# Moving low parts and the sine products of a rotation from GpSimd to VectorE in one layer of a decoder trunk

## The chip, the cores and the metric

The kernel runs on one core of one Trainium2 chip. The metric is the device time of one execution in microseconds, the median of several runs. The engines are named as in the profile: PE is TensorE (PEld its weight loads), DVE is VectorE, ACT is ScalarE, POOL is GpSimd, SP is SyncE, which issues most transfers.

## The reference

One layer of a trunk is computed for 2048 prompt rows and 8 single sample rows of width 1024, all in 32-bit floats:

```python
mod = (jax.nn.silu(c) @ w_ada + b_ada)[:, None, :]
sh1, sc1, g1, sh2, sc2, g2 = jnp.split(mod, 6, axis=-1)
h = modulate(x, norm1_g, sh1, sc1)          # rmsnorm(x, gain) * (1 + scale) + shift
u, q, k, v, a_pool, a_attn = project_inputs(h, pos, w_in, q_norm_g, k_norm_g)
# q, k: per-head rmsnorm, then rope:
#   concatenate([x1 * cos - x2 * sin, x2 * cos + x1 * sin], axis=-1)
pool_y = pool_mix(ext, pos, w_pool_grp, pool_scale)
# three groups of 4 heads with (window, dilation) = (128,1), (512,4), (2048,16)
attn_y = combine_groups(outs, lses)
merged = sigmoid(a_pool) * (pool_y @ w_pool_br) + sigmoid(a_attn) * (attn_y @ w_attn_br)
x = x + g1 * (merged @ w_out)
h2 = modulate(x, norm2_g, sh2, sc2)
x = x + g2 * (jnp.square(jax.nn.relu(h2 @ w_up)) @ w_down)
```

## The kernel before

Everything is held transposed, with features on the 128 partitions and positions along the free dimension. The positions are worked in two groups (`ci` 0: 1024 prompt rows and the 8 sample rows; `ci` 1: the other 1024 prompt rows), each in two halves of 512 or 520 columns.

Products keep the precision of 32-bit floats by splitting each operand into a high part, which is the value rounded to the matmul's type (fp32r), and a low part, which is the rest. A matmul becomes three (high x high, high x low, low x high), added up in PSUM (`mm3`, L156). So every weight tile is loaded by SyncE into a raw buffer, cast by ScalarE to its high part, and a subtraction makes its low part (`load_w`, L178 to 185). Its default engine is GpSimd (`eng=G`); the tiles of `w_ada` have VectorE. `weights` (L213) hands the tiles out in the order of `plan` (L188 to 207) and asks for the next one or two ahead of use (`depth`), and passes GpSimd. There are three raw buffers and three for the parts. The same split is made for the modulated rows h and h2 in `modulated` (L317): VectorE multiplies x by the reciprocal root, ScalarE scales and shifts, ScalarE casts the high part, and the low part is made on GpSimd for odd k and on VectorE for even k (calls at L360 and L1252).

The stages are: an opening (L748), in which the first blocks of `w_ada`, the norm of x and the first q/k tiles are made as the data lands; the first group's q/k/v projection (`qkv`, L393), gates with the rest of `w_ada` and the sample rows' attention beside them, the pooling branch (L530); the second group's pooling branch; its q/k/v projection with the attention of all heads interleaved (L929 to 1141); its gates with the merging of the heads; then for each group the output projection (`project`, L1254), the second norm (`norm2`, L1246), and the two feed-forward products (`up`, `down`), which take the second half of the time.

In `qkv` each chunk of q or k is copied out of PSUM by ScalarE as a pair of half-heads `a`, `b` and as squares. `after_qk` (L400) then adds the two squares on GpSimd (L405), makes the products with sine on GpSimd (L409, L411) and with cosine on VectorE (L410, L412), a difference and a sum on VectorE (L413, L414), and some microseconds later the norm over a head by a small matmul, square root and reciprocal (L416 to 422). The result is split into high and low parts in `ohl` (one buffer; ScalarE L444, GpSimd L445) and stored; the attention reads it back later.

TensorE's order of work is written out by hand: the class `Order` (L65) keeps a running estimate of TensorE's time and steps through generators with delays, so that small matmuls and other stages are laid between the large ones. The order on each of the other engines' queues is chosen when the program is built, by priority; `first()` (L149) raises it, for weights (L182) and for the copies out of PSUM. On each engine instructions run in their queue's order.

Of the kernel before, what the change touches and what calls it, by code (L numbers as in the profile page):

```python
# [8 lines left out]
F32 = mybir.dt.float32  # L9
F32R = mybir.dt.float32r  # L10
AF = mybir.ActivationFunctionType
ALU = mybir.AluOpType
# [4 lines left out]
P = 128  # L17
# [97 lines left out]
def emit(tc, I, O):  # L115
    nc = tc.nc
    V, S, G, PE, SP = nc.vector, nc.scalar, nc.gpsimd, nc.tensor, nc.sync
# [90 lines left out]
    ready = []  # L208
    extra = []
    issued = [0]  # L210
    depth = [DEPTH]

    def weights(*key):  # L213

        i = issued[0] - len(ready)
        assert plan[i] == key, (plan[i], key)
        while issued[0] < len(plan) and issued[0] <= i + depth[0]:
            k = plan[issued[0]]
            src = I[k[0]][k[1]] if len(k) == 2 else I[k[0]][k[1], :, k[2] * 1024:(k[2] + 1) * 1024]
            ready.append(load_w(src, G, *(extra if issued[0] == 3 else ())))  # L220
            issued[0] += 1
        return ready.pop(0)

# [5 lines left out]
    for name, shape in CPACK:  # L229
        n = int(np.prod(shape))  # L230
# [83 lines left out]
            V.reciprocal(out=rs[:, c0:c0 + n], in_=rs[:, c0:c0 + n])  # L314
        return rs

    def modulated(hf, x, xr, rs, n, i, k, dst, c0, samp, eng):  # L317

        sh = (0 if i == 0 else 24) + k
        V.tensor_tensor(out=xr, in0=x, in1=rs[:, :n], op=ALU.mult)  # L320
        S.activation(out=hf[:, :n], in_=xr, func=AF.Identity, scale=sc[:, i, k, 0:1], bias=mod[:, sh, 0:1])
        if samp:
            sl = slice(n - NS, n)
            V.tensor_tensor(out=hf[:, sl], in0=xr[:, sl], in1=sc[:, i, k, 1:9], op=ALU.mult)
            V.tensor_tensor(out=hf[:, sl], in0=hf[:, sl], in1=mod[:, sh, 1:9], op=ALU.add)
        S.copy(out=dst[:, k, 0, c0:c0 + n], in_=hf[:, :n])
        eng.tensor_tensor(out=dst[:, k, 1, c0:c0 + n], in0=hf[:, :n], in1=dst[:, k, 0, c0:c0 + n].bitcast(F32), op=ALU.subtract)  # L327


    ph1 = ExitStack()  # L330
# [25 lines left out]
    def make_h(ci, hi, xs, rs, hb, ks=range(KD)):  # L356
        c0, n, splits = HALVES[ci][hi]
        for k in ks:
            hf = npl.tile([P, 520], F32, tag="sq", bufs=3, name="hf")
            modulated(hf, xs[k], xs[k], rs, n, 0, k, hb, c0, ci == 0 and hi == 1, G if k % 2 else V)  # L360

    def subs(ci):
        out = []
# [29 lines left out]
    def qkv(ci, hb, done=None):  # L393
        st = ExitStack()
        opened = None if ci else opening()
        ap = pool(st, f"qkv{ci}", side="left")
# [3 lines left out]
        def after_qk(g, qk, t0, n, ab, sq):  # L400
# [5 lines left out]
            a, b, co, si = ab[:, 0, :n], ab[:, 1, :n], cs[:, 0, :n], cs[:, 1, :n]  # L406
            t = ap.tile([P, 2, 512], F32, tag="rt", bufs=1, name="rt")
            o = ap.tile([P, 2, 512], F32, tag="ro", bufs=2, name="ro")
            G.tensor_tensor(out=t[:, 0, :n], in0=b, in1=si, op=ALU.mult)  # L409
            V.tensor_tensor(out=o[:, 0, :n], in0=a, in1=co, op=ALU.mult)  # L410
            G.tensor_tensor(out=t[:, 1, :n], in0=a, in1=si, op=ALU.mult)  # L411
            V.tensor_tensor(out=o[:, 1, :n], in0=b, in1=co, op=ALU.mult)  # L412
            V.tensor_tensor(out=o[:, 0, :n], in0=o[:, 0, :n], in1=t[:, 0, :n], op=ALU.subtract)  # L413
            V.tensor_tensor(out=o[:, 1, :n], in0=o[:, 1, :n], in1=t[:, 1, :n], op=ALU.add)  # L414
# [5 lines left out]
            V.reciprocal(out=rs[:, :n], in_=rs[:, :n])  # L420
            for i in range(2):
                V.tensor_tensor(out=o[:, i, :n], in0=o[:, i, :n], in1=rs[:, :n], op=ALU.mult)
            ohl = ap.tile([P, 2048], F32R, tag="ohl", bufs=1, name="ohl")
            dst = (kst if qk else qst)[g]
            for i in range(2):
                oi = o[:, i, :npr]
# [819 lines left out]
    def norm2(ci, hi, acc, hb, xa):  # L1246
        c0, n, splits = HALVES[ci][hi]
        yield 2500
        rs = rms_finish(tp, stp, acc, splits)
        for k in range(KD):  # L1250
            hg, hf = wtile("hg"), wtile("hf")
            modulated(hf, xa[k][:, c0:c0 + n], hg[:, :n], rs, n, 1, k, hb, 0, ci == 0 and hi == 1, G if k % 2 else V)  # L1252

    def project(ci, hi, hb, xa, load_xa=None):  # L1254
        c0, n, splits = HALVES[ci][hi]
# [65 lines left out]
    for ci in range(2):  # L1321
# [4 lines left out]
        xa = []  # L1326
# [9 lines left out]
        accs = tp.tile([P, KD, NS], F32, tag="accs", bufs=1, name="accs") if ci == 0 else None  # L1336
        br = od.spawn(branches(ci, 1, hbs[1], GAP_B), 3000)
        depth[0] = DEPTH_O
        acc = project(ci, 0, hbs[0], xa, load_xa)
        od.drain(br)  # L1340
        n0 = od.spawn(norm2(ci, 0, acc, hbs[0], xa))
# [139 lines left out]
```

## Time and profile before

| | |
|---|---|
| median of 3 runs | 3063.06 us (3058.80 to 3064.57) |
| profiled execution | 3062.32 us |
| its span, first to last instruction | 3060.5 us |
| TensorE busy | 2933.8 us, 96% |
| VectorE busy | 1590.5 us, 52% |
| ScalarE busy | 982.3 us, 32% |
| GpSimd busy | 966.2 us, 32%, of which 649.3 us at L184 |
| chain that ended last, by engine | PE 76%, DMA 5%, DVE 5%, issue 4%, POOL 3%, ACT 2% |

Busy shares are means over stages with different limits. The time of a matmul includes part of its neighbours' time, since they are pipelined. An idle time is put down to what ended it. "issue" is time in which an engine waited for nothing that the profile shows.

### The profile page before, as it was taken

To read this page: it belongs to the slowest core of one execution; us is meant where nothing else is said; L and a number is where in the kernel's file an instruction comes from. 1 tells how busy PE (TensorE), PEld (TensorE's weight loads), DVE (VectorE), ACT (ScalarE), POOL (GpSimd) and SP (SyncE) were. 2 spreads that over 40 slices of the span, in tenths; PEclk is the share of its full clock that TensorE was granted. 3 is DMA by queue.
4 is the path that set the end of the run, shared out by engine and by line. 5 is a ranking of instruction groups with operands and counts; after the bars stand their busy time and mean duration, and the time that the engine had idled before them with its cause. 6 is when DMAs were issued, how large, how long until landed. Compare 5 with 4: busy or idle time off the path is not lost.

```text
span 3060.5 us, 40917 instructions
## 1 busy us (share of the span) xinstructions
PE 2933.8 (96%) x16220; PEld 2510.3 (82%) x16220; DVE 1590.5 (52%) x2649; ACT 982.3 (32%) x1772; POOL 966.2 (32%) x510
## 2 busy tenths in 40 slices
PE   6899999999898799999999999999999999999999
PEld 3899788887787688878899999999877888888887
DVE  5556442541744534456865545555677554444444
ACT  5333342433554534433521221121235211111211
POOL 2665341433533312233532122122245312221221
PEclk7999999999999889999999999999999999999999
DMA  6544752335777779876321111111272211111111
GB/s 239 172 144 154 270 183 92 118 118 151 200 196 203 186 191 229 239 243 218 105 78 48 43 49 49 42 51 47 92 242 83 76 42 56 48 49 42 55 43 69
DMA packets 207599, 379.09 MB, mean 124 GB/s; under 512 B 47424, under 2 KB 103072, under 8 KB 206624
## 3 DMA queue, kind: packets, MB, share of 16 engines
q1 hardware_dynamic: 195888, 359.63, 38.6%
q10 hardware_dynamic: 11520, 16.85, 1.5%
q8 instruction: 128, 2.10, 0.3%
q14 instruction: 63, 0.52, 0.1%
HBM read 294.89 MB, written 81.75 MB: 123 GB/s over the span
## 4 chain that ended last, share of the span: by engine, by line
PE 76%; DMA 5%; DVE 5%; issue 4%; POOL 3%; ACT 2%; SPq 1%; ACTq 0%; DVEq 0%; POOLq 0%
PE ps_dn L153 23%; PE ps_up L153 22%; PE ps_g L153 10%; PE ps_v L153 4%; PE ps_qk L153 4%; PE ps_wo L153 3%; PE ps_u L153 3%; PE ps_o L153 1%; PE ps_pb L153 1%; POOL wh L184 1%; PE ps_s L153 1%; PE ps_ada L153 1%; DMA slab<-kst 1%; DMA cs<-in_rope 1%; PE ps_ab L153 1%
## 5 line engine op out<-in xcount | busy, mean ns | idle before, releaser
L184 POOL TENSOR_TENSOR wh<-wr,wh 128x1024 fp32r<-128x1024 f32 (+1 forms) x274 | 649.3, 2377 | 1637.9 <-ACT wh L183 1620.7
L153 PE MATMUL ps_dn<-rt,wh 128*128 128x512 f32 (+2 forms) x3840 | 727.0, 350 | 5.3 <-POOL wh L184 3.3
L153 PEld LDWEIGHTS ps_dn<-rt,wh 128*128 128x128 f32 x3840 | 619.6, 188 | 108.2 <-POOL wh L184 4.2
L183 ACT CAST wh<-wr 128x1024 fp32r<-128x1024 f32 (+1 forms) x306 | 309.4, 1023 | 737.9 <-issue 564.0
L1306 DVE SCALAR_TENSOR_TENSOR xa<-ps_dn,mod,xa 128x512 f32<-128x512 f32 (+1 forms) x640 | 405.2, 642 | 202.1 <-PE ps_dn L153 195.9
L153 PE MATMUL ps_g<-h,wh 128*128 128x512 f32 (+2 forms) x1920 | 389.6, 354 | 0.4 <-POOL wh L184 0.4
L153 PE MATMUL ps_up<-hb,wh 128*128 128x264 f32 (+2 forms) x2304 | 371.7, 319 | 0.0
L153 PE MATMUL ps_up<-ha,wh 128*128 128x512 f32 x1536 | 367.3, 395 | 0.0
L153 PEld LDWEIGHTS ps_up<-hb,wh 128*128 128x128 f32 x2304 | 332.3, 188 | 36.1
L153 PEld LDWEIGHTS ps_g<-h,wh 128*128 128x128 f32 x1920 | 307.2, 190 | 48.5 <-POOL wh L184 1.0
L153 PEld LDWEIGHTS ps_up<-ha,wh 128*128 128x128 f32 x1536 | 286.6, 188 | 66.3 <-issue 0.5
L153 PE MATMUL ps_qk<-h,wh 128*128 128x512 f32 (+2 forms) x1440 | 301.4, 362 | 14.2 <-POOL wh L184 4.9
L1290 DVE TENSOR_TENSOR r<-r 128x512 f32<-128x512 f32 (+2 forms) x160 | 99.3, 621 | 389.2 <-ACT r L1289 389.1
L153 PEld LDWEIGHTS ps_qk<-h,wh 128*128 128x128 f32 x1440 | 233.6, 193 | 58.5 <-POOL h L327 6.3
L1292 DVE TENSOR_TENSOR rt<-r,rt 128x512 fp32r<-128x512 f32 (+2 forms) x160 | 218.0, 1362 | 81.7 <-ACT rt L1291 81.6
L1289 ACT ACTIVATE r<-ps_up 128x512 f32<-128x512 f32 (+2 forms) x160 | 82.1, 513 | 416.8 <-PE ps_up L153 416.8
L153 PE MATMUL ps_v<-wh,h 128*128 128x256 f32 (+1 forms) x1224 | 171.6, 297 | 25.4 <-ACT wh L183 19.3
L153 PEld LDWEIGHTS ps_v<-wh,h 128*128 128x128 f32 (+1 forms) x1224 | 157.8, 195 | 30.5 <-ACT wh L183 19.7
L945 ACT ACTIVATE pe<-pe,ost 128x128 f32<-128x128 f32 (+1 forms) x192 | 87.1, 454 | 142.5 <-DVE ost L943 139.5
L943 DVE CUSTOM_DVE_ANT_0 pe<-ps_s,cp 128x128 f32<-128x128 f32 (+1 forms) x192 | 61.5, 358 | 118.2 <-PE ps_s L153 118.0
L1291 ACT CAST rt<-r 128x512 fp32r<-128x512 f32 (+2 forms) x160 | 85.7, 536 | 66.4 <-DVE r L1290 66.4
L445 POOL TENSOR_TENSOR ohl<-ro,ohl 128x256 fp32r<-128x256 f32 (+1 forms) x66 | 76.1, 1175 | 92.4 <-ACT ohl L444 81.8
(182 smaller groups left out, 2981.7 us busy)
## 6 DMA issues: line engine op xcount, KB each, us to landing
wr<-in_w_up SPq DMA_DIRECT2D x72, 512.0 KB
wr<-in_w_down SPq DMA_DIRECT2D x68, 512.0 KB
wr<-in_w_in SPq DMA_DIRECT2D x64, 512.0 KB
wr<-in_w_ada SPq DMA_DIRECT2D x48, 512.0 KB
slab<-kst SPq DMA_DIRECT2D x40, 512.0 KB
wr<-in_w_out SPq DMA_DIRECT2D x32, 512.0 KB
cs<-in_rope SPq DMA_DIRECT2D x18, 512.0 KB
qst<-ohl SPq DMA_DIRECT2D x9, 1024.0 KB
```

Source lines behind the costliest of these rows:

```text
L153: PE.matmul(ps, w, x, start=start, stop=stop)
L183: S.copy(out=wt[:, 0, :n], in_=raw[:, :n])
L184: eng.tensor_tensor(out=wt[:, 1, :n], in0=raw[:, :n], in1=wt[:, 0, :n].bitcast(F32), op=ALU.subtract)
L445: G.tensor_tensor(out=pl, in0=pi, in1=ph.bitcast(F32), op=ALU.subtract)
L943: V.tensor_tensor_reduce(out=pe[:, off:off + nk], in0=ps[:, off:off + nk], in1=mask[:, mo:mo + nk], scale=-0.125, scalar=3.0e38, op0=ALU.a ...
L945: S.activation(out=pe[:, off:off + nk], in_=pe[:, off:off + nk], func=AF.Exp, scale=-1.0, bias=o[:, 64:65], accum_out=o[:, 65:66])
L1289: S.activation(out=r1[:, :l], in_=ps[:, :l], func=AF.Relu)
L1290: V.tensor_tensor(out=r1[:, :l], in0=r1[:, :l], in1=r1[:, :l], op=ALU.mult)
L1291: S.copy(out=rt[:, 0, a:a + l], in_=r1[:, :l])
L1292: V.tensor_tensor(out=rt[:, 1, a:a + l], in0=r1[:, :l], in1=rt[:, 0, a:a + l].bitcast(F32), op=ALU.subtract)
L1306: V.scalar_tensor_tensor(out=x[:, c0 + a:c0 + a + lp], in0=ps[:, :lp], scalar=mod[:, 40 + m, 0:1], in1=x[:, c0 + a:c0 + a + lp], op0=ALU.m ...
```

## The change

Three kinds of operations go from GpSimd to VectorE. In `weights` the engine of the low part becomes a variable, VectorE until the first group's output projection begins, and GpSimd from there on (the tiles of `w_attn_br`, loaded in `branches`, keep the default). In `modulated` the low part is always on VectorE. In `after_qk` both sine products are on VectorE. Besides, `ohl` has two buffers in the first group and one, as before, in the second.

```diff
+    weng = [V]
...
-            ready.append(load_w(src, G, *(extra if issued[0] == 3 else ())))
+            ready.append(load_w(src, weng[0], *(extra if issued[0] == 3 else ())))
...
-    def modulated(hf, x, xr, rs, n, i, k, dst, c0, samp, eng):
+    def modulated(hf, x, xr, rs, n, i, k, dst, c0, samp):
...
-        eng.tensor_tensor(out=dst[:, k, 1, c0:c0 + n], in0=hf[:, :n], in1=dst[:, k, 0, c0:c0 + n].bitcast(F32), op=ALU.subtract)
+        V.tensor_tensor(out=dst[:, k, 1, c0:c0 + n], in0=hf[:, :n], in1=dst[:, k, 0, c0:c0 + n].bitcast(F32), op=ALU.subtract)
...
-            modulated(hf, xs[k], xs[k], rs, n, 0, k, hb, c0, ci == 0 and hi == 1, G if k % 2 else V)
+            modulated(hf, xs[k], xs[k], rs, n, 0, k, hb, c0, ci == 0 and hi == 1)
...
-            G.tensor_tensor(out=t[:, 0, :n], in0=b, in1=si, op=ALU.mult)
+            V.tensor_tensor(out=t[:, 0, :n], in0=b, in1=si, op=ALU.mult)
             V.tensor_tensor(out=o[:, 0, :n], in0=a, in1=co, op=ALU.mult)
-            G.tensor_tensor(out=t[:, 1, :n], in0=a, in1=si, op=ALU.mult)
+            V.tensor_tensor(out=t[:, 1, :n], in0=a, in1=si, op=ALU.mult)
...
-            ohl = ap.tile([P, 2048], F32R, tag="ohl", bufs=1, name="ohl")
+            ohl = ap.tile([P, 2048], F32R, tag="ohl", bufs=2 - ci, name="ohl")
...
-            modulated(hf, xa[k][:, c0:c0 + n], hg[:, :n], rs, n, 1, k, hb, 0, ci == 0 and hi == 1, G if k % 2 else V)
+            modulated(hf, xa[k][:, c0:c0 + n], hg[:, :n], rs, n, 1, k, hb, 0, ci == 0 and hi == 1)
...
         depth[0] = DEPTH_O
+        weng[0] = G
         acc = project(ci, 0, hbs[0], xa, load_xa)
```

## Rows read from the trace of the kernel before

**Rows 1.** Busy us of PE, PEld, DVE, ACT, POOL by stretch; clock; DMA
```profile
0.00:125.00 125.00, 90.51 (x480) 67.00 (x481) 73.71 (x101) 59.73 (x103) 55.30 (x43) 0.85 0.54 197
125.00:750.00 625.00, 608.86 (x3666) 524.42 (x3666) 276.05 (x364) 228.41 (x364) 257.25 (x153) 0.99 0.47 155
750.00:1150.00 400.00, 349.70 (x2015) 308.97 (x2014) 193.31 (x442) 189.84 (x445) 142.39 (x85) 0.93 0.78 198
1380.00:3060.50 1680.50, 1660.39 (x8840) 1420.57 (x8838) 938.09 (x1339) 411.24 (x628) 450.25 (x197) 1.00 0.22 74
```

**Rows 2.** Groups by shape, GpSimd to 1380 us, then VectorE: busy us, mean ns
```profile
L184 POOL TENSOR_TENSOR wh<-wr,wh 128x1024 fp32r<-128x1024 f32 x89 | 218.6, 2460 | 444.6 <-ACT wh L183 442.1 <-issue 2.4
L409 POOL TENSOR_TENSOR rt<-ab,cs 128x512 f32<-128x512 f32 x18 | 28.7, 1597 | 42.8 <-ACT ab L390 24.1 <-DMA cs<-in_rope 18.7
...
L413 DVE TENSOR_TENSOR ro<-ro,rt 128x264 f32<-128x264 f32 x6 | 2.6, 426 | 0.0
```

**Rows 3.** Timeline of VectorE and GpSimd: start us, length us, operation, idle before
```profile
311.98 1.23 DVE L184 TENSOR_TENSOR wh<-wr,wh 128x1024 fp32r<-128x1024 f32 x1 [2.35 <-ACT wh L183]
...
78.20 0.69 DVE L410 TENSOR_TENSOR ro<-ab,cs 128x512 f32<-128x512 f32 x1
...
83.47 1.71 POOL L405 TENSOR_TENSOR qsq<-qsq 128x512 f32<-128x512 f32 x1
83.99 1.75 DVE L414 TENSOR_TENSOR ro<-ro,rt 128x512 f32<-128x512 f32 x1
```

**Rows 4.** Timeline of TensorE in the opening, with what ended its idle time
```profile
39.35 3.72 PE L153 MATMUL ps_qk<-h,wh 128*128 128x512 f32 x8 [3.21 <-POOL wh L184]
...
54.97 4.63 PE L153 MATMUL ps_qk<-h,wh 128*128 128x512 f32 x10 [1.69 <-POOL wh L184]
...
86.93 5.60 PE L153 MATMUL ps_qk<-h,wh 128*128 128x256 f32 x32 [3.88 <-POOL h L327]
...
120.51 0.71 PE L153 MATMUL ps_hs<-qsq,cp 128*128 128x264 f32 x2 [2.52 <-POOL qsq L405]
```

**Rows 5.** Timeline of GpSimd, ScalarE and VectorE ahead of those four waits
```profile
33.30 3.23 POOL L327 TENSOR_TENSOR h<-hf,h 128x512 fp32r<-128x512 f32 x1 [32.87 <-ACT h L326]
...
43.36 1.16 ACT L305 ACTIVATE sq<-x 128x520 f32<-128x520 f32 x2 [3.71 <-POOL h L327]
...
51.13 3.42 DVE L314 RECIPROCAL rs<-rs 128x256 f32<-128x256 f32 x2 [1.36 <-ACT rs L313]
...
85.15 1.72 POOL L327 TENSOR_TENSOR h<-hf,h 128x520 fp32r<-128x520 f32 x1
...
118.85 0.91 POOL L411 TENSOR_TENSOR rt<-ab,cs 128x256 f32<-128x256 f32 x1
```

**Rows 6.** Timeline of TensorE from 750 to 1150 us, three of its waits
```profile
882.10 1.08 PE L153 MATMUL ps_o<-vt,px 128*128 128x64 f32 x8 [1.19 <-DVE ost L963]
...
925.80 4.42 PE L153 MATMUL ps_v<-wh,h 128*128 128x256 f32 x19 [2.77 <-POOL wh L184]
...
1068.82 0.79 PE L153 MATMUL ps_v<-wh,h 128*128 128x256 f32 x2 [16.22 <-ACT wh L183]
```

**Rows 7.** Timeline of VectorE and GpSimd ahead of the first two
```profile
878.26 3.49 DVE L422 TENSOR_TENSOR ro<-ro,qrs 128x512 f32<-128x512 f32 x2
878.26 2.93 POOL L184 TENSOR_TENSOR wh<-wr,wh 128x1024 fp32r<-128x1024 f32 x1 [2.64 <-ACT wh L183]
...
922.95 2.79 POOL L184 TENSOR_TENSOR wh<-wr,wh 128x1024 fp32r<-128x1024 f32 x1
```

**Rows 8.** Chain that ended last, around the third: start, length, what
```profile
1060.50 0.57 SPq L456
```

**Rows 9.** Timeline of VectorE and TensorE near 350 us
```profile
350.85 4.47 DVE L184 TENSOR_TENSOR wh<-wr,wh 128x1024 fp32r<-128x1024 f32 x2
354.25 1.47 PE L153 MATMUL ps_ada<-wh,silr 128*18 128x512 f32 x3 [3.82 <-DVE wh L184]
```

**Rows 10.** GpSimd's waits from 750 to 1150 us: what, total us, times, longest
```profile
POOL wh L184 <- ACT wh L183: 85.9, 8, 31.6
```

## Prediction

> **What bounds the kernel now.** I read four views in this order: the busy times by stretch, the timeline of TensorE with what ended its idle time, the timelines of the engines named there, and the groups by shape for prices. The stretches [rows 1] show a kernel that TensorE fills: after 1380 us it is busy 1660.39 of 1680.50 us, and little that VectorE or GpSimd do there can return time. Its idle time lies in two places, 34.5 us in the first 125 us (the opening) and 50.3 us from 750 to 1150 us (the second q/k/v projection, between whose matmuls the attention runs). From 125 to 750 us it idles 16.1 us. So the change is worth what it takes out of waits in the opening and in 750 to 1150 us, at most some 85 us, and much of that is first loads and waits on other engines.
>
> GpSimd is a slow place for these operations and it slows VectorE as well. A 128x1024 low part takes 2.46 us on GpSimd in the mean of 89, a sine product of 512 columns 1.60 us [rows 2]; VectorE, alone, does a 128x1024 low part in 1.23 us [rows 3]. A 128x512 operation takes 0.69 us on VectorE alone, but when GpSimd has one at the same moment the two take 1.75 and 1.71 us [rows 3]. That pair is done after about 1.73 us; both on VectorE would take 1.38.
>
> **The moved work.** Counted from the code: 87 weight low parts (42 of the first group, 44 of the second, and the first output-projection tile, fetched before the switch at L1340); 32 of the 64 low parts of modulated rows (odd k), 16 before 1150 us and 16 after 1380; 60 sine products (30 chunks of two), 36 of 512 columns and 24 of 256 or 264. On VectorE, alone: 87 x 1.23 = 107 us, 32 x 0.69 = 22 us, 36 x 0.69 + 24 x 0.43 = 35 us (0.43 from a sum of 264 columns [rows 2]). That is 164 us, of which 138 fall before 1150 us (75 weights, 16 rows, all products), where VectorE is busy 543 of 1150 us [rows 1]. It comes to 59%, less what it gains by fewer collisions; 750 to 1150 us goes from 193 to some 240 of 400 us, the opening from 74 to some 95 of 125 us (7 weights, 8 rows, 12 products). No stretch becomes full. GpSimd loses over 300 us. Busy time is not the question; order and latency are. Each moved low part still waits for ScalarE's cast (L183, L326), now in VectorE's queue, where the copies of ps_v (L510), ps_o (L963) and the score reductions (L943) stand behind it; TensorE waits for all three.
>
> **The opening, step by step** [rows 4].
> (a) At 39.35 us TensorE resumes after 3.21 us, released by a weight's low part. GpSimd had first spent 3.23 us on a modulated row, from 33.30, and came to the weights at 36.5 [rows 5]. On VectorE this low part follows its cast by 1.23 us. The gain is at least 1.5 us (three normalisations of 0.69 us may stand in front) and at most 3.7 us, because the squares of the second half also stood 3.71 us behind GpSimd's row [rows 5]. I take 3.
> (b) At 54.97 us the next weight ends a wait of 1.69 us. On VectorE it meets two reciprocals, 3.42 us from 51.13 [rows 5]: ahead of them it gains 1.2 us, behind them it comes at 55.8 and loses 0.8. I take 0.
> (c) At 86.93 us TensorE has waited 3.88 us for the last modulated row, which GpSimd did from 85.15 in 1.72 us, behind other work [rows 5]. On VectorE right after its cast it comes 3.8 us sooner; with the six operations of a rotation in front (6 x 0.69 = 4.1 us, from about 79.5) some 3 us sooner. I take 3.5.
> (d) At 120.51 us it has waited 2.52 us for the sum of squares (L405), which stays on GpSimd but stood behind the two products, the second at 118.85 [rows 5]. Without them, some 0.8 us each: 1.6 us, bounds 0.5 and 2.5.
> Sum 8.1 us, bounds 4 and 11. After 125 us TensorE is nearly full (608.86 of 625 us), so what is gained stays gained unless loads hold it up later. The second ohl buffer frees ScalarE from waiting for stores in this part; TensorE's own work hides that, and where it did not the buffer could only gain: 0.
>
> **750 to 1150 us** [rows 6].
> (e) At 925.80 TensorE waited 2.77 us for a value weight's low part, which took GpSimd 2.79 us [rows 7] and VectorE 1.23: 1.5 us less. One more such wait follows at 1071.25 (about 1 us less). 2.5 us; 0 if VectorE is amid a rotation each time.
> (f) At 882.10 it waited 1.19 us for a copy of attention output, one of three such waits within 20 us. The copy stood behind two normalisations that took 3.49 us while GpSimd did a weight in 2.93 us [rows 7]. Alone the two take 1.38; with the weight's 1.23 in front 2.6. So 0.9 us each, 2.5 in all; bounds 0 and 3.5.
> (g) The longest wait, 16.22 us at 1068.82, is for a value weight that landed late. Its transfer stood on SyncE's queue behind the store of rotated keys, which went at 1060.50 [rows 8]. That store ends a rotation that began late through TensorE's own order, so most of the wait stays. Four products in a row on VectorE (2.8 us) against two on each engine at once (3.4 us) bring it forward 0.6 us; bounds 0 and 2.
> Sum 5.6 us, bounds 0 and 8.
>
> **What it costs elsewhere.** (h) Around 350 us two low parts of w_ada took VectorE 4.47 us, because GpSimd did a weight beside them, and TensorE waited for them [rows 9]. Now that weight stands in the same queue: one low part more, +1.2 us; bounds -1 (three at 1.23 are 3.7 us) and +3. Between 560 and 640 us eight modulated rows join VectorE's pooling chain, 8 x 0.69 = 5.5 us, spread over 80 us in which it is half busy: 0, bounds -1 and +3. After 1380 us the 16 rows add 11 us to a VectorE that is busy 938 of 1680 us [rows 1], while GpSimd is the sooner free for its weights: 0, bounds -2 and +3.
>
> **The sum.** -8.1 - 5.6 + 1.2 = -12.5 us. The profiled execution took 3062.32 us, 3060.5 of them its span; it lies 0.7 us below the median of 3063.06. So 3062.3 - 12.5 + 0.7 = 3050.5 us, and with the bounds of the terms, not all at once, 3042 to 3060. TensorE's granted clock averages 0.85 of full in the opening, a mixture of its levels of 1.2 and 2.4 GHz, and 0.99 in the next stretch [rows 1]; shorter waits could raise it, and I count nothing for that.
>
> **The rivals.**
> One, only the opening: from 750 to 1150 us loads and TensorE's own order set the end of every wait, as in (g), and VectorE's new work takes back (e) and (f). Time: 3063.06 - 8.1 + 1.2 = 3056. For it: that stretch keeps the DMA engines 78% busy [rows 1].
> Two, a trade without profit: work moved between two engines that get in each other's way frees as much as it costs. Then (c) to (g) go, since VectorE is busy at those moments, and (a), where it had idle time, stays: 3063.06 - 3 + 1.2 = 3061. Against it: 1.73 us for the pair against 1.38 [rows 3].
> The Trainium skill (Perfetto Trace Analysis, section "Optimizing Scalar/DVE Operations") states the rule behind this rival: GpSimd and VectorE share a port to SBUF, so offloading between them might not help. The pair in the trace agrees that they slow each other, and disagrees that nothing is left to win in this direction.
> Three, slower: VectorE's queue is held by weights. The order of that queue is fixed when the program is built; where a load is later than planned, the copies out of PSUM behind the low part wait, and TensorE with them. GpSimd stood idle 85.9 us for casts in 750 to 1150 us [rows 10], harmless while it had nothing else to do. If a quarter of that, 21 us, falls on VectorE ahead of copies that TensorE needs, the time is 3056 + 21 = 3077. It decides once such holds pass about 14 us. Against it: ScalarE queues behind the same loads already, and the latest weight, in (g), is one that TensorE waits for anyway.
>
> **How the numbers follow.** Forecast 3050.5 with 0.53; rival one 0.17; rival two 0.15; rival three 0.15. A measurement of this kernel tells about 0.2%, 6.1 us, from no change. The forecast and rival one lie beyond that, rival one by 1 us only, so 0.03 of it goes to "same": faster 0.67, same 0.18, slower 0.15. The range reaches from 3037, all gains at their far bounds (11 + 8 us) and some clock, to 3067, which leaves out most of rival three.
>
> **What would show it.** In the profile after, TensorE's waits at about 39, 87 and 120 us are gone or below 1 us and the first value matmuls come some 8 us earlier; VectorE's 128x512 operations come near 0.7 us and its weights take 1.2 to 1.5 us; the wait of 16 us is still there. The prediction is wrong if VectorE stands idle before L184 from 750 to 1150 us with copies of ps_v or ps_o late behind it (rival three), if VectorE's mean times are unchanged (rival two), or if new waits of TensorE on loads eat the opening's gain.

## The result, and the profile after

The changed kernel takes 3020.36 us (median of 5 runs, 3015.57 to 3023.81) against 3063.06 us before: a ratio of 0.9866, 95% interval 0.9851 to 0.988. That is 42.7 us less, where 12.5 were forecast, and it lies below the range of 3037 to 3067. The direction was right; the size was not. Its profiled execution took 3020.36 us, its span 3018.6.

The busy times of the page of the changed kernel, two of its groups, and the busy times by stretch (PE, PEld, DVE, ACT, POOL, then clock, DMA share, GB/s), to be held against [rows 1, 2]. Lines after L213 stand one further down than before, after L1340 two.

```profile
PE 2927.0 (97%) x16220; PEld 2507.5 (83%) x16220; DVE 1666.0 (55%) x2828; ACT 984.5 (33%) x1772; POOL 638.3 (21%) x331
...
L184 POOL TENSOR_TENSOR wh<-wr,wh 128x1024 fp32r<-128x1024 f32 (+1 forms) x187 | 435.5, 2338 | 1294.7 <-ACT wh L183 1284.7
...
L184 DVE TENSOR_TENSOR wh<-wr,wh 128x1024 fp32r<-128x1024 f32 x119 | 160.4, 1353 | 140.6 <-ACT wh L183 138.3
```
```profile
0.00:125.00 125.00, 99.92 (x615) 78.23 (x616) 90.90 (x150) 62.78 (x110) 22.26 (x24) 0.92 0.65 230
125.00:750.00 625.00, 614.09 (x3632) 527.84 (x3630) 326.18 (x438) 235.23 (x376) 102.33 (x65) 0.99 0.47 155
750.00:1150.00 400.00, 368.85 (x2160) 325.95 (x2160) 215.09 (x560) 199.79 (x478) 61.89 (x44) 0.94 0.82 209
```

In the first 125 us TensorE now starts 615 matmuls where it started 480, and from 750 to 1150 us 2160 where it was 2015. VectorE is busy 632 of the first 1150 us, 55%, close to the 59% counted. No stretch of it became full.

**Where the time went.** Both kernels issue the same 16220 matmuls in the same order. So the start of the n-th matmul of one can be compared with that of the other, and their difference is the time won up to that point. Worked out so from the two traces, in us, at times of the kernel before:

```
up to          125     400     900    1000    1080    1300     end
after         -15.8   -19.9   -17.6   -24.4   -50.0   -34.9   -42.0
```

The opening won 15.8 us (forecast 8.1). Then 26 us went at one place, 1000 to 1080 us, where 0.6 was forecast. Of that, 15 came back before 1300 us. Another 7 went after 1300 us, where nothing was forecast; some 3 of these 7 are most likely not the change's (see (h) below).

TensorE's timeline in the opening answers to [rows 4]: the waits of 3.21, 1.69 and 3.88 us are 0.56, 0.75 and 0.91; the one for the sum of squares at 120.51 has no idle time at all now (106.38).

```profile
35.98 4.46 PE L153 MATMUL ps_qk<-h,wh 128*128 128x512 f32 x10 [0.56 <-DVE wh L184]
...
50.04 2.32 PE L153 MATMUL ps_qk<-h,wh 128*128 128x512 f32 x5 [0.75 <-DVE wh L184]
...
76.98 3.21 PE L153 MATMUL ps_qk<-h,wh 128*128 128x256 f32 x25 [0.91 <-DVE h L328]
...
106.38 0.61 PE L153 MATMUL ps_hs<-qsq,cp 128*128 128x264 f32 x2
```

TensorE's timeline in the second projection answers to [rows 6]. The wait of 16.22 us is gone: that matmul starts at 1024.20 with no wait. In its place stand three that were shorter before (none, 2.29 and 4.66 us ahead of the same matmuls), for a copy of attention output and for slabs of stored keys: the last three lines.

```profile
871.31 1.10 PE L153 MATMUL ps_o<-vt,px 128*128 128x64 f32 x8 [2.31 <-DVE ost L964]
...
905.33 2.50 PE L153 MATMUL ps_v<-wh,h 128*128 128x256 f32 x19 [0.76 <-DVE wh L184]
...
1044.50 1.94 PE L153 MATMUL ps_o<-vt,px 128*128 128x64 f32 x8 [3.66 <-DVE ost L964]
...
1060.73 2.14 PE L153 MATMUL ps_s<-slab 128*128 128x128 f32 x8 [2.83 <-DMA slab<-kst]
...
1098.09 1.19 PE L153 MATMUL ps_s<-slab 128*128 128x256 f32 x4 [6.00 <-DMA slab<-kst]
```

Why the 16 us went is on SyncE's queue. First its timeline in the kernel before, around the store of [rows 8], then in the changed kernel:

```profile
988.18 0.42 SPq L180 DMA_DIRECT2D wr<-in_w_v  x1
...
1060.50 0.57 SPq L456 DMA_DIRECT2D kst<-ohl  x1
1061.12 0.62 SPq L180 DMA_DIRECT2D wr<-in_w_v  x1
```
```profile
962.90 1.18 SPq L180 DMA_DIRECT2D wr<-in_w_v  x2
```

Before, the first w_v weight of the last group is fetched at 988, and the second stands behind the store of rotated keys until 1061. After, both are fetched together at 963. The code of these loads is the same in both kernels; their place in SyncE's queue is chosen when the program is built, and the planner chose another one. It moved other transfers of the queue too: of the four loads of w_in that stood behind the w_v load at 1061 us before, the first goes at 1028.69 now, ahead of the key store.

### The profile page after: what moved, and what is told of

The parts are those of the page before. It is cut to its first block, busy times and chain, and to the rows that moved or that the text cites. A ratio compares the mean times of both kernels' runs of the same rounds, so it can differ in the third digit from the quotient of the medians.

```text
span 3018.6 us, 40807 instructions
## 1 busy us (share of the span) xinstructions
PE 2927.0 (97%) x16220; PEld 2507.5 (83%) x16220; DVE 1666.0 (55%) x2828; ACT 984.5 (33%) x1772; POOL 638.3 (21%) x331
## 4 chain that ended last, share of the span: by engine, by line
PE 83%; DMA 5%; DVE 5%; issue 3%; ACT 2%; POOL 2%; SPq 1%; ACTq 0%; DVEq 0%; POOLq 0%
PE ps_up L153 24%; PE ps_dn L153 23%; PE ps_g L153 9%; PE ps_qk L153 7%; PE ps_v L153 4%; PE ps_u L153 3%; PE ps_pb L153 3%; PE ps_wo L153 2%; PE ps_o L153 2%; PE ps_s L153 1%; POOL wh L184 1%; DMA slab<-kst 1%; PE ps_ada L153 1%; PE ps_t L172 1%; DMA kc<-in_kc 1%
## 5 line engine op out<-in xcount | busy, mean ns | idle before, releaser
L184 POOL TENSOR_TENSOR wh<-wr,wh 128x1024 fp32r<-128x1024 f32 (+1 forms) x187 | 435.5, 2338 | 1294.7 <-ACT wh L183 1284.7
L1307 DVE SCALAR_TENSOR_TENSOR xa<-ps_dn,mod,xa 128x512 f32<-128x512 f32 (+1 forms) x640 | 405.2, 641 | 202.4 <-PE ps_dn L153 197.3
L1293 DVE TENSOR_TENSOR rt<-r,rt 128x512 fp32r<-128x512 f32 (+2 forms) x160 | 215.5, 1347 | 80.4 <-ACT rt L1292 80.2
L184 DVE TENSOR_TENSOR wh<-wr,wh 128x1024 fp32r<-128x1024 f32 x119 | 160.4, 1353 | 140.6 <-ACT wh L183 138.3
L406 POOL TENSOR_TENSOR qsq<-qsq 128x512 f32<-128x512 f32 (+2 forms) x30 | 38.3, 1278 | 366.0 <-ACT qsq L392 366.0
```

The lines of the kernel that those rows point to most:

```text
L184: eng.tensor_tensor(out=wt[:, 1, :n], in0=raw[:, :n], in1=wt[:, 0, :n].bitcast(F32), op=ALU.subtract)
L406: G.tensor_tensor(out=sq[:, 0, :n], in0=sq[:, 0, :n], in1=sq[:, 1, :n], op=ALU.add)
L1293: V.tensor_tensor(out=rt[:, 1, a:a + l], in0=r1[:, :l], in1=rt[:, 0, a:a + l].bitcast(F32), op=ALU.subtract)
L1307: V.scalar_tensor_tensor(out=x[:, c0 + a:c0 + a + lp], in0=ps[:, :lp], scalar=mod[:, 40 + m, 0:1], in1=x[:, c0 + a:c0 + a + lp], op0=ALU.m ...
```

## The experiments

All twelve were compared with runs of the kernel before on the same chip. The table gives the median, the ratio with its interval, that ratio as us of 3063, and where SyncE issues the second w_v load of the last group: "late" is right behind the key store, "early" beside the first.

```
run                          median    ratio [95%]               us     load
the change                   3020.36   0.9866 [0.9851, 0.988]   -41.0   early
e1_weights                   3045.12   0.995  [0.9934, 0.9966]  -15.3   late
e2_rotation                  3054.11   0.9976 [0.9966, 0.9986]   -7.4   late
e3_rows                      3056.77   0.9991 [0.9979, 1.0004]   -2.8   late
e4_load_early                3056.54   0.9988 [0.9977, 0.9999]   -3.7   early
e5_one_weight_back           3028.33   0.9891 [0.9869, 0.9913]  -33.4   late
e6_all_but_rows              3032.14   0.9903 [0.9883, 0.9923]  -29.7   early
e7_all_but_weights           3048.62   0.9958 [0.9945, 0.997]   -12.9   late
e8_all_but_rotation          3038.61   0.9923 [0.9907, 0.994]   -23.6   late
e9_after_stores_gpsimd       3007.79   0.9832 [0.9815, 0.985]   -51.5   early
e10_before_stores_gpsimd     3034.19   0.9916 [0.9901, 0.9931]  -25.7   early
e11_all_weights_vector       3011.75   0.9845 [0.9825, 0.9864]  -47.5   early
e12_both                     2995.49   0.9787 [0.9769, 0.9804]  -65.2   early
```

And the time won up to a matmul, as above, from the profiled execution of each. A row is one execution, so its end can lie some 8 us from the ratio (e7: -21.0 against -12.9).

```
up to          125     400     900    1000    1080    1300     end
e1             -6.5    -7.3    +2.8   -12.1   -16.8   -14.8   -16.3
e2             -4.6    -7.5    +6.6    -4.5    -5.2    -4.9    -8.5
e3             +3.0    +0.3    +1.7    +0.4    +0.6    +2.6    -4.2
e4             -0.4    -1.8    +1.1    -2.3   -20.2    -3.3    -6.5
e5            -14.6   -16.6   -12.4   -19.8   -24.2   -22.9   -27.4
e6            -11.5   -16.8   -12.9   -21.1   -46.7   -31.2   -25.6
e7             -8.2   -11.3    -1.4   -11.6   -12.7   -12.8   -21.0
e8             -7.2    -6.1    +1.9   -11.1   -16.5   -15.2   -22.1
e9            -15.0   -18.0   -18.9   -31.6   -53.6   -52.3   -58.4
e10            -0.8    -3.2    +0.2   -10.1   -28.4   -26.6   -27.9
e11           -16.0   -17.5   -17.9   -27.2   -51.8   -38.5   -55.1
e12           -12.6   -11.9   -11.3   -25.6   -48.2   -48.7   -65.9
```

**One part at a time, and the load's place alone.** The first theory was that the 42 us are the opening plus the load's new place at its full 16 to 22 us.

```diff
 e1, on before:
-            ready.append(load_w(src, G, *(extra if issued[0] == 3 else ())))
+            ready.append(load_w(src, weng[0], *(extra if issued[0] == 3 else ())))
 (with weng = [V] at the top and weng[0] = G at the output projection, as in the change)
 e2, on before:
-            G.tensor_tensor(out=t[:, 0, :n], in0=b, in1=si, op=ALU.mult)
+            V.tensor_tensor(out=t[:, 0, :n], in0=b, in1=si, op=ALU.mult)
-            G.tensor_tensor(out=t[:, 1, :n], in0=a, in1=si, op=ALU.mult)
+            V.tensor_tensor(out=t[:, 1, :n], in0=a, in1=si, op=ALU.mult)
 e3, on before, at both calls of modulated:
-            modulated(hf, xs[k], xs[k], rs, n, 0, k, hb, c0, ci == 0 and hi == 1, G if k % 2 else V)
+            modulated(hf, xs[k], xs[k], rs, n, 0, k, hb, c0, ci == 0 and hi == 1, V)
 e4, on before, in load_w:
-        SP.dma_start(out=raw[:, :n], in_=src)
+        with (first() if early else ExitStack()):
+            SP.dma_start(out=raw[:, :n], in_=src)
 (early for the second w_v load of the last group of the second half alone)
```

Expected of e1: 

> Only the weights' low parts go to VectorE; rows, rotation and the ohl buffer stay as before. In this kernel SyncE's queue keeps the second w_v load of the last q/k/v group of the second half behind the store of rotated keys. Theory 1 (the 16 us wait went because that load is issued ahead of the store): the wait of 16 us near 1069 us stays; the opening gains most of its 17 us (three waits for weights, 10 to 13 us), the waits near 340 and 925 us some 4 to 6: 3043 to 3050 us. Rival 2 (the wait went because the weights left GpSimd, whatever the queue): the wait is gone already here, 3022 to 3030 us.

Expected of e2: 

> Only the two sine products of the rotation go to VectorE. The load stays behind the store here too. Theory 1: the 16 us wait stays, nothing of the opening's weights changes; within 4 us of before (3059 to 3065). Rival 3 (the rotation ends sooner on one engine, its store leaves SyncE sooner, and so the load behind it): the wait near 1069 us shrinks by 8 us or more, 3050 us or less.

Expected of e3: 

> Only the modulated rows' low parts go to VectorE. The load stays behind the store. Theory 1: the wait of 16 us stays; the wait for the last row near 87 us shrinks by some 3 us and nothing else: 3057 to 3062 us. Rival (the opening's gain comes from the rows, which no longer hold up the weights on GpSimd): the opening gains 10 us or more, 3047 to 3053 us.

Expected of e4: 

> No instruction changes its engine. Only the second w_v load of the last group of the second half is given precedence, so that SyncE issues it right behind the first w_v load, some 100 us sooner, ahead of the rotation's table loads and key stores. Theory 1: the wait of 16 us near 1069 us (and the 2 us one behind it) goes without any work moved; some of it is given back at the later waits for slabs: 3041 to 3050 us. Rival 2 (it is the work taken off GpSimd): the cast and low part of this weight are as slow as before, the wait moves to them and nearly all of it stays: 3058 to 3063 us.

In e1 to e3 the load is late and the wait is there. TensorE's timeline in e1, with SyncE's beside it, then TensorE's in e2:

```profile
1053.20 0.79 PE L153 MATMUL ps_v<-wh,h 128*128 128x256 f32 x2 [16.40 <-ACT wh L183]
...
1044.70 0.57 SPq L457 DMA_DIRECT2D kst<-ohl  x1
1045.32 0.62 SPq L180 DMA_DIRECT2D wr<-in_w_v  x1
```
```profile
1063.60 0.80 PE L153 MATMUL ps_v<-wh,h 128*128 128x256 f32 x2 [15.38 <-ACT wh L183]
```

So rival 2 falls: in e1 the weight's low part is on VectorE and the wait is as long as ever. Rival 3 falls with e2, where the wait lost about 1 us and not 8. The load's place decides the wait, and no single part moves it: it is late with the weights alone and with the rotation alone, and early with both (e6).

But e4 also contradicts the first theory, by its price. The load is issued early, the wait of 16 us is gone without any work moved, and the kernel is 3.7 us faster where 13 to 22 were expected. Its row in the table says why: 18 us won between 1000 and 1080 us, 17 of them lost again by 1300. In e4 SyncE issues the load at 985, and TensorE meets new waits:

```profile
985.12 1.93 SPq L181 DMA_DIRECT2D wr<-in_w_v  x2
...
1015.25 2.15 PE L153 MATMUL ps_s<-slab 128*128 128x128 f32 x8 [4.71 <-DMA slab<-kst]
...
1074.87 1.51 PE L153 MATMUL ps_o<-vt,px 128*128 128x64 f32 x6 [4.23 <-DVE ost L964]
...
1128.46 1.19 PE L153 MATMUL ps_s<-slab 128*128 128x256 f32 x4 [6.49 <-DMA slab<-kst]
```

The stall had been a cover: while TensorE stood, the slabs and the copy that it needs next came in. Without it they come too late. e1 gave the 15 us expected, but the opening gave 6.5 of them and not 10 to 13; and e2 gave 7.4, more than expected (within 4), 4.6 of it in the opening. e3, whose interval includes no change, met its expectation of a few us, but not where it was expected: 0.4 us were lost up to 1000 us and 6.8 won after 1300.

**The changed kernel less one part.** A fourth theory took the first one's place: the load's new place is worth little after what comes back, and in the opening the parts help each other, since they shared one queue.

```diff
 e5, on the changed kernel:
-            ready.append(load_w(src, weng[0], *(extra if issued[0] == 3 else ())))
+            ready.append(load_w(src, G if issued[0] == 64 else weng[0], *(extra if issued[0] == 3 else ())))
 (64 is the second w_v weight of the middle group of the second half)
```

e6, e7 and e8 each undo one of the hunks above: the rows, the weights, the rotation; e7 and e8 keep the second ohl buffer, and so does e6.

Expected of e5: 

> The changed kernel with one single low part back on GpSimd, that of the second w_v weight of the middle group of the second half. With it the planner puts the load of the next group's second w_v weight back behind the store of rotated keys in SyncE's order, as in the kernel before. Theory 1 (the load's place is worth what it takes away at 1069 us): the wait of 16 us is back at full price, 3036 to 3042 us. Theory 4 (the load's place removes some 18 us at that spot, but three quarters come back in the next 200 us as waits for slabs of stored keys and for ost, as the run with the early load alone showed): 3022 to 3030 us.

Expected of e6: 

> The change without its part on the modulated rows. Theory 4 (the parts of the opening share GpSimd's queue, a wait there ends only when all that stands ahead on it is gone): the wait of 4 us for the last row near 77 us comes back with more than its own 1.2 us, the opening gains 10 to 12 of the 17 us, the load stays early: 3024 to 3029 us. Rival (the parts add: rows alone gave 0 to 4): 3020 to 3024 us.

Expected of e7: 

> The change without its part on the weights; the load goes back behind the store of keys. Theory 4: the opening keeps 5 to 8 of its 17 us, the waits near 340 and 925 us come back in part, the wait of 16 us is back, and with it the waits for slabs behind it are less: 3040 to 3050 us. Rival (the parts add; rotation and rows alone gave 6.7 and 4.1): 3050 us.

Expected of e8: 

> The change without its part on the rotation; the load goes back behind the store of keys. Theory 4: the opening keeps 10 to 12 of its 17 us, the wait of 16 us is back, less waiting for slabs behind it: 3030 to 3040 us. Rival (the parts add; weights and rows alone gave 15.7 and 4.1): 3041 us.

e5 shows the load's place best. One low part of 119 back on GpSimd, that of a weight loaded at 901 us, puts the load back behind the store, and the wait is back. TensorE's and SyncE's timelines in e5:

```profile
1045.90 0.80 PE L153 MATMUL ps_v<-wh,h 128*128 128x256 f32 x2 [15.66 <-ACT wh L183]
...
1037.24 0.57 SPq L457 DMA_DIRECT2D kst<-ohl  x1
1037.86 0.62 SPq L180 DMA_DIRECT2D wr<-in_w_v  x1
```

The time is 3028.33 us, as the fourth theory said and not the first: the load's place is worth 7.6 us (41.0 less 33.4), not 16. The two intervals overlap, and together they allow about 0 to 16 us; but the same matmuls say nearly the same. From 900 to 1300 us the change won 17.3 us and e5 10.5. The opening's 14.6 us and the rest stay. Moving one low part also moved other transfers in SyncE's order, so the 7.6 us are the load's place with what came along.

e7 and e8 came out as the fourth theory said (3048.62 in 3040 to 3050, 3038.61 in 3030 to 3040), but the adding of single parts said nearly the same, so they don't tell the two apart; and e8's opening kept 7.2 us, not 10 to 12. e6 missed both: 3032.14 us, where 3024 to 3029 or 3020 to 3024 were expected. The table places it. Without the rows the opening ends at -11.5 and not at -15.8, as the fourth theory said, and the stretch after 1300 us loses 5.6 us (in one execution, the slowest of its four). Over the runs: from 1300 us to the end, the kernels with the rows on VectorE and later weights on GpSimd win 7.1, 6.8, 4.5, 8.2, 6.9 and 6.1 us (the change, e3, e5, e7, e8, e9), those with the rows on both engines 1.5, 3.6, 3.2 and 1.3 and a loss of 5.6 (e1, e2, e4, e10, e6). That is 6.6 against 0.8 in the mean, or against 2.4 without e6; (h) below shows the two places where it lies. e6 also tells that the second ohl buffer, which it has, is worth little in the opening: e1 and e2, which have its other two parts and one buffer, won 11.1 us there together.

The early load in e6 came with weights, rotation and the second buffer; that the buffer has no part in it was not tested.

**Whose queue.** If what comes back comes from slabs that stand behind a waiting store in SyncE's queue, the stores should leave it.

```diff
 e9, on the changed kernel, and e10, on the kernel before, at both places:
-                SP.dma_start(out=dst[:, :, t0:t0 + npr], in_=ohl[:, :4 * npr].bitcast(F32).rearrange("p (c n) -> p c n", c=4))
+                (G if ci else SP).dma_start(out=dst[:, :, t0:t0 + npr], in_=ohl[:, :4 * npr].bitcast(F32).rearrange("p (c n) -> p c n", c=4))
 e11, on the changed kernel (e12 has this and e9):
-        weng[0] = G
```

The first line stands for both stores of the second half. Expected of e9: 

> The changed kernel, and in the second half the stores of rotated queries and keys are issued from GpSimd's queue, right behind the low part that GpSimd itself writes into them, in place of SyncE's queue. Theory 5 (what came back after the wait of 16 us went are loads of slabs that stand in SyncE's queue behind a store that waits for the rotation: SyncE waits 12.5 us there between 1020 and 1105 us): the waits for slabs near 936, 988, 1061 and 1098 us (1.9, 1.2, 3.0 and 6.2 us) go or shrink to half: 3009 to 3016 us. Rival (those slabs wait for the stored keys themselves: matmul, rotation, store and load in a row, whoever issues them): 3018 to 3022 us.

Expected of e10: 

> The kernel before with the same stores issued from GpSimd's queue; no arithmetic moves. The second w_v load of the last group comes early by itself. Theory 5: the wait of 16 us goes as with the early load alone, and less comes back as waits for slabs: 3045 to 3053 us. Rival (GpSimd's queue is the fuller one here, 40 per cent busy in this half against 21 in the changed kernel, so the stores and with them the slabs come later): 3055 to 3066 us.

Expected of e11: 

> The changed kernel without the switch back to GpSimd at the output projection: the low parts of all later weights go to VectorE too. Theory (TensorE waits for GpSimd's weight parts at three places after 1330 us, 5.8 us in all, and VectorE has room, 54 to 59 per cent busy): 3014 to 3018 us. Rival (VectorE carries residuals, squares and drains in an order that now has a weight ahead at each step; 187 instructions of 1.2 us more): 3022 to 3035 us.

Expected of e12: 

> The two edits before this one together on the changed kernel: stores of the second half from GpSimd's queue, all weights' low parts on VectorE. They touch different stretches (900 to 1150 us, and after 1330 us), so the gains should add: 3005 to 3014 us. Rival: with both, the later stretch loses what the earlier gains: 3018 to 3024 us.

e9 takes 3007.79 us (by its ratio 3011.6 of 3063, within the 3009 to 3016 expected), 10.5 less than the change by the ratios. Between 1080 and 1300 us it gives back 1.3 us, where the change gave back 15.1. First SyncE's longest waits in the changed kernel from 1020 to 1110 us (what, total us, times, longest):

```profile
SPq L990 <- DVE ost L964: 16.4, 6, 7.7
SPq L457 <- POOL ohl L446: 12.5, 2, 8.3
...
```

In e9 the wait of L457 is not on SyncE. GpSimd issues the store itself, 0.30 us after its own low part (GpSimd's timeline, then TensorE's):

```profile
1038.87 1.28 POOL L446 TENSOR_TENSOR ohl<-ro,ohl 128x512 fp32r<-128x512 f32 x1 [1.28 <-ACT ohl L445]
1040.44 0.73 POOL L457 DMA_DIRECT2D kst<-ohl  x1 [0.30 <-POOL ohl L446]
...
1086.44 1.19 PE L153 MATMUL ps_s<-slab 128*128 128x256 f32 x4 [4.93 <-DMA slab<-kst]
```

And TensorE over the same 1267 matmuls, busy times as in [rows 1], in the kernel before (220 us), in the changed kernel (235.1 us) and in e9 (221.3 us):

```profile
1080.00:1300.00 220.00, 212.60 (x1266) 187.58 (x1266) 91.07 (x395) 92.42 (x259) 43.99 (x24) 0.98 0.88 221
```
```profile
1030.00:1265.10 235.10, 219.75 (x1267) 194.10 (x1266) 101.31 (x421) 96.60 (x270) 23.41 (x16) 0.93 0.89 227
```
```profile
1026.40:1247.70 221.30, 212.59 (x1267) 187.63 (x1266) 95.28 (x414) 93.55 (x267) 21.98 (x15) 0.98 0.90 227
```

So of the 15 us that came back in the changed kernel, 8.0 are idle time (7.4 to 15.4) and 7.2 are matmuls that ran at a mean granted clock of 0.93 instead of 0.98: more stops, more stretches at the lower of the two levels (behind the wait that ended at 1044.50 the clock was 0.50 from 1045 to 1050 us). e9 has nearly the figures of before: 6.6 us less idle time than the change (15.4 to 8.7), and 7.2 us less for the matmuls. Of the four waits for slabs, those near 936 and 988 us are gone; that of 2.83 us is 1.85 in e9, and that of 6.00 is 4.93, which is not the half that theory 5 asked for. The transfer behind the last one is under way for 10.20 us in the chain of the changed kernel.

```profile
1087.76 10.20 DMA slab<-kst
```

The largest part of the 6.6 us is no slab: the wait of 3.66 us at 1044.50 for a copy of attention output (L964), which in the changed kernel stood on VectorE's queue behind a reciprocal, two normalisations and score reductions.

```profile
1038.35 3.35 DVE L421 RECIPROCAL qrs<-qrs 128x512 f32<-128x512 f32 x1
...
1043.93 0.42 DVE L964 COPY ost<-ps_o 128x256 f32<-128x256 f32 x1
```

In e9 that matmul does not wait; VectorE makes a copy right behind the reciprocal there. So theory 5 is shown for a part, and the rest came with another order on VectorE.

e10 surprised most. Without moving any arithmetic, the stores on GpSimd's queue, with the order that the planner makes of it, bring the kernel before to 3034.19 us, 25.7 us less, two thirds of what the whole change brought, and beyond either expectation. Both w_v loads come at 976.68 there, and the 28.4 us won by 1080 are kept (26.6 at 1300). The load's early place alone was worth 3.7 us (e4). Other loads moved too: the second w_v weight of the middle group is fetched at 859 us in e10, where it went at 913 before (at 837 in e9, at 896 in the changed kernel). So how much of the 25.7 us is the queue itself, and how much the earlier loads, is not told apart.

e11 takes 3011.75 us, 6.5 us below the change by the ratios (3015.6 of 3063, within the theory's 3014 to 3018). The intervals of the two overlap, but those of e12 and e9, which differ by the same edit, do not. The groups of VectorE from 1300 to 2990 us, shapes apart, in the changed kernel and then in e11 (count, busy us, mean ns):

```profile
L1307 DVE SCALAR_TENSOR_TENSOR xa<-ps_dn,mod,xa 128x512 f32<-128x512 f32 x368 | 270.7, 747 | 148.9 <-PE ps_dn L153 147.7
L1293 DVE TENSOR_TENSOR rt<-r,rt 128x512 fp32r<-128x512 f32 x95 | 128.4, 1351 | 52.3 <-ACT rt L1292 52.1
```
```profile
L1307 DVE SCALAR_TENSOR_TENSOR xa<-ps_dn,mod,xa 128x512 f32<-128x512 f32 x375 | 276.9, 749 | 163.6 <-PE ps_dn L153 163.3
L184 DVE TENSOR_TENSOR wh<-wr,wh 128x1024 fp32r<-128x1024 f32 x172 | 207.3, 1221 | 33.3 <-ACT wh L183 32.5 <-DMA t<-t1d 0.5
...
L1293 DVE TENSOR_TENSOR rt<-r,rt 128x512 fp32r<-128x512 f32 x96 | 66.2, 689 | 38.5 <-ACT rt L1292 38.5
```

VectorE takes on 172 weights, 207 us, and is busy 968 us of these 1690 where it was 956. Several of its own operations with two operands in SBUF became that much shorter: L1293 gives back 62 us in the form shown and 121 in its three forms together. L1307, which reads PSUM, stays at 747 to 749 ns. e12, both edits together, takes 2995.49 us and is the fastest kernel of the study: 0.9787 of before (0.9769 to 0.9804), 24.2 us below the change, where the two alone sum to 17.0; the intervals are wide enough for plain adding. It beat its expectation of 3005 to 3014.

## Why the prediction was wrong, point by point

**(a) to (d), the opening: right mechanism, too small.** The four waits fell by 2.65, 0.94, 2.97 and 2.52 us, 9.1 in all, against 3, 0, 3.5 and 1.6. None was off by more than a microsecond; at (b) the low part came between the two reciprocals, behind one of them. In all, TensorE's waits for GpSimd fell from 14.2 to 1.1 us, while those for weights and rows on VectorE rose from 0.6 to 3.0 and those for ScalarE's casts of weights from 3.9 to 5.4. The step that failed is the sentence on the clock, "I count nothing for that". The changed kernel's busy times over the first 480 matmuls, which took 125 us before:

```profile
0.00:109.20 109.20, 84.12 (x480) 63.00 (x481) 80.88 (x128) 59.35 (x103) 16.41 (x18) 0.91 0.60 219
```

Against [rows 1], 9.4 of the 15.8 us are idle time (34.5 to 25.1), and the other 6.4 are shorter matmuls, at a mean granted clock of 0.91 instead of 0.85. How much of the 6.4 belongs to the change is not shown. In e5, e9, e11 and e12, which have all its parts in the opening, the idle time falls by 9.4 to 10.8 us, and the matmuls take 2.4 to 6.6 us less. Nor do shorter waits always bring a higher clock: e2 has 5.7 us less idle time and a clock of 0.82, and its matmuls take about 1 us more.

Counting each part alone would have missed it too: e1 to e3 win 6.5, 4.6 and -3.0 us there, 8.1 together, and five kernels with all parts 12.6 to 16.0. But the idle time adds up: 2.7, 5.7 and 0.5 us, 8.9 together, against 9.4 to 10.8. So what the parts seemed to do for each other is mostly the clock, and the fourth theory's reason, the shared queue, is not shown. In e3, with only the rows off GpSimd, TensorE's waits for its sums of squares rose to 6.6 us, and the matmuls ran at 0.82.

**(e) and (f): held.** The value weight's wait went from 2.77 to 0.76 us [rows 6]. Of the three waits for ost near 890 us, which were 1.19, 1.46 and 1.18, two are all but gone and one is 2.31; from matmul to matmul the three are 1.3 us shorter, and a fourth, of 0.74 us at 946, is gone. That is 2.0 and some 2 us against 2.5 and 2.5.

**(g): the step that failed.** "Most of the wait stays" took SyncE's order as given and asked only how soon its store could go. The prediction itself said that the order of a queue is fixed when the program is built, and did not draw from it that moved work gives the planner another program to order. The wait went whole, by the load's place. Net it was worth 7.6 us (e5), because much of what was won there came back: against e5, the change won 21 us from 1000 to 1080 us and lost 14 by 1300. Had I foreseen the load's place, I would have counted 16 to 18 us for it, too much for that term; e4 shows 3.7 for it alone.

**(h): too dark.** Near 350 us +1.2 us were forecast; the table shows a gain of 4.1 from 125 to 400 us, but e4 and e10, which move no arithmetic, won 1.4 and 2.4 there. The wait of 3.82 us [rows 9] belonged to that one execution of before: at the same matmul it is 0.68 us in e4 and none in e10, which leave these low parts where they were. TensorE's waits for these two weights of w_ada sum to 6.2 us before, 4.4 in e4, 4.0 in e10 and 0.75 in the changed kernel. TensorE's timeline in e4, then in the changed kernel:

```profile
353.70 0.87 PE L153 MATMUL ps_ada<-wh,silr 128*18 128x512 f32 x3 [0.68 <-DVE wh L185]
```
```profile
326.91 0.88 PE L153 MATMUL ps_ada<-wh,silr 128*18 128x512 f32 x3 [0.75 <-DVE wh L184]
```

After 1380 us 0 was forecast, with -2 as bound, and 5.0 us were won by the rows: with the clock, the second term that was put at nothing. They lie at two places, 2.3 us from 1500 to 1600 us and 2.7 from 2350 to 2400 (times of before), where the second norm of each group's second half runs beside the first feed-forward products. All six kernels with the rows on VectorE and later weights on GpSimd win just these, and e1, e2, e4, e6 and e10 at most 0.3 at either. TensorE's timeline at the first place, before and after: one wait, for VectorE's sums into x, is gone, and the other is shorter.

```profile
1515.19 9.03 PE L153 MATMUL ps_dn<-rt,wh 128*128 128x512 f32 x37 [1.59 <-POOL wh L184]
1525.73 1.66 PE L153 MATMUL ps_dn<-rt,wh 128*128 128x512 f32 x6 [1.51 <-DVE xa L1306]
```
```profile
1478.15 10.26 PE L153 MATMUL ps_dn<-rt,wh 128*128 128x512 f32 x43 [1.29 <-POOL wh L184]
```

Another 3.1 us lie from 1420 to 1460 us, and e1, e2, e4 and e10, whose rows stay as before, have 2.8 to 3.2 of them: they are not the rows', and most likely belong to the profiled execution of before.

**The sum.** By the table, with (f), which lies near 890 us, in the second stretch: opening -15.8 against -8.1, 125 to 900 us -1.8 against -1.3, 900 to 1300 us -17.3 against -3.1, the rest -7.1 against 0; -42.0 in all against -12.5. No term came out much smaller than forecast, and three were missing: the clock behind a wait, another place in a queue, and the later half.

**The rivals.** Rival one fell with (e) to (g). Rival two fell by VectorE's means, in the kernel before and then after:

```profile
L422 DVE TENSOR_TENSOR ro<-ro,qrs 128x512 f32<-128x512 f32 x36 | 39.2, 1132 | 0.1
L413 DVE TENSOR_TENSOR ro<-ro,rt 128x512 f32<-128x512 f32 x18 | 27.8, 1547 | 15.7 <-POOL rt L409 15.7
```
```profile
L423 DVE TENSOR_TENSOR ro<-ro,qrs 128x512 f32<-128x512 f32 x36 | 25.2, 735 | 0.0
L414 DVE TENSOR_TENSOR ro<-ro,rt 128x512 f32<-128x512 f32 x18 | 13.4, 745 | 0.0
```

They came near 0.7 us, as forecast. The price held against that rival was misread, though: the two operations of [rows 3] overlap for 1.2 us only and are both done 2.27 us after the first began, not 1.73. The Trainium skill's rule behind that rival (Perfetto Trace Analysis, section "Optimizing Scalar/DVE Operations": moving work between GpSimd and VectorE might not help) is not what these runs show in this direction: e11 moved 207 us of work from one to the other and VectorE's busy time grew by 12. Rival three did not come: from 750 to 1150 us VectorE waited 7.2 us for casts of weights, 2.5 at most, where GpSimd had waited 85.9 [rows 10].

```profile
DVE wh L184 <- ACT wh L183: 7.2, 7, 2.5
```

**What stays open.** Why the planner's choice flips with weights and rotation together, and with a single weight in e5, was seen in the queues and not traced further. The wait of 5 to 6 us for a slab near 1098 us stays in e9 and e12 (4.93 and 4.82); nothing was tried against it, nor against the waits of L990 on SyncE, which are longer than those of L457. The second ohl buffer was not run alone. Why the opening's clock differs between kernels with nearly the same idle time stays open, and so does how much of e9 and e10 comes from the new order of other loads.

## What to carry to other kernels

Where queues are ordered by a planner, a moved instruction can change the place of a transfer far from it: compare the order of the DMA queue before and after, not only the engines' times. Ask of a long stall what it hides; here 15 of 26 us came back, and no longer did once the stores that wait for other engines had left the queue of the loads (e9). And where two engines slow each other, price the moved work by what it gives back to the engine that takes it.

## What the runs showed of the hardware

The place of issue was worth nearly two thirds as much as the whole change. Putting the second half's stores on the queue of the engine that writes their data (e10) won 25.7 us without moving any arithmetic, together with the new order of loads that came with it. The Trainium skill (Trainium Kernel Development and Optimization, section "Key Constraints") says that issuing from several engines saves only the sequencer's issue time; these runs show more, since a store that waits holds the loads behind it: 12.5 us on SyncE in 90 us of the changed kernel. Its warning of transfers issued by GpSimd while VectorE holds the ports that the two share (SBUF — State Buffer, section "SBUF: two separate sides", the box on the "DVE blocks DMA" trap) did not tell here: the eight stores of L457 in e9 took 0.73 to 0.74 us each to issue, and the kernel won. Whether VectorE held the ports at such a moment is not shown.

With 512 columns, VectorE's operation L1293 took 1351 ns beside GpSimd's weights and 689 without them, with the same shape in the same place; L1307, which reads PSUM, took 747 and 749.
